# Cross entropy with label smoothing: one sum and one exponential per transfer, the first row completed on GpSimd, fewer instructions on VectorE and ScalarE

## The chip, the cores and the metric

One core of one Trainium2 chip. The time is device microseconds of one execution; medians of repeated runs are quoted. The profile is one execution on the chip, with times counted from the start of its span (first to last instruction of the kernel). The time is 1.7 to 1.9 us longer than the span (in every run but those of e2_old_end), since a closing sequence follows it. Engines: PE is TensorE (PEld its weight loads), DVE is VectorE, ACT is ScalarE, POOL is GpSimd, SP issues transfers.

## The reference, cut to what matters

```
batch, num_classes = 256, 32000          # logits fp32: 32.77 MB
log_probs = logits - max; log_probs -= log(sum(exp(log_probs)))
smooth_targets = smoothing/num_classes everywhere, + (1 - smoothing) at the label
return -sum(smooth_targets * log_probs)  # one number per row
```

The kernel needs, per row, the sum of the logits, the sum of their exponentials and the logit at the label. Each of 128 partitions holds two rows, handled one after the other. All 32.77 MB are read once.

## The kernel before

Each row is read in transfers of the widths below. Wide ones land in a ring of three buffers, narrow ones in buffers of their own. Every landed tile is cut into pieces of at most 4032 columns; each piece gets one sum on VectorE and one exponential with accumulation on ScalarE.

```
WIDTHS = (
    (8000, 8000, 8000, 8000),
    (8000, 6272, 4736, 3648, 2688, 2048, 1536, 1216, 1024, 832),
)
RING_MIN = 6000
PIECE = 4032
...
        if w >= RING_MIN:
            xt = ring.tile([P, max(WIDTHS[0])], FP32, name="xt", tag="xt")
        else:
            xt = tail.tile([P, w], FP32, name=name, tag=name)
...
    def sum_exps(xp, w: int, out: bass.AP) -> None:
        ja = turn.tile([P, PIECE], BF16, name="ja", tag="ja")   # three buffers
        nc.scalar.activation(out=ja[:, :w], in_=xp, func=AF.Exp, accum_out=out)
...
    # last row, at its last two tiles
        elif left == 1:
            nc.vector.tensor_tensor(
                out=done[1][:], in0=done[0][:], in1=pairs[0][:], op=ALU.add
            )
            nc.gpsimd.tensor_tensor(
                out=se_rest[:], in0=done[1][:, 1:2], in1=pairs[1][:, 1:2], op=ALU.add
            )
        elif left == 0:
            nc.vector.tensor_tensor(
                out=lin[:], in0=done[1][:, 0:1], in1=pairs[1][:, 0:1], op=ALU.add
            )
...
    finish(r, lin[:], elast[:], se_rest[:])   # logarithm, two transposes, combination
```

The softmax here doesn't subtract the row's maximum and nothing guards it: scores larger than these inputs give would overflow.

## Time and profile before

| | before |
|---|---|
| time, median | 85.11 us (85.00 to 85.12, 3 runs) |
| span of the profiled run | 83.23 us |
| instructions in the built program: VectorE, ScalarE, TensorE, GpSimd, SyncE | 78, 69, 50, 37, 37 |
| last tile landed, result landed, end of span | 78.92, 82.19, 83.23 us |

The instruction counts are from the built program, accumulator reads, waits and markers included. The landings are the semaphore records of the trace. Two lines of the page of the kernel before, busy time by engine and the busy tenths of the DMA engines in 40 slices of the span:

```profile
PE 8.0 (10%) x20; PEld 5.4 (6%) x20; DVE 38.7 (47%) x52; ACT 59.9 (72%) x45; POOL 4.6 (6%) x15
DMA  5999998996999699988999799999999999999500
```

No compute engine is busy for three quarters of the span, and the DMA engines are busy nearly everywhere but in the last two slices.

### The profile page before, as it was taken

Reading aid. Unit: us, or ns where it says so; the run is one execution under the profiler, and the core shown is the slowest. Engines: PE = TensorE matmul, PEld = TensorE weight load, DVE = VectorE, ACT = ScalarE, POOL = GpSimd, SP = SyncE. Lnnn points to the kernel's source line nnn. Section 1 sums busy time; section 2 is a strip of 40 time slices with the busy share of each in tenths; the row PEclk is TensorE's granted clock in tenths of the full one; section 3 lists DMA queues with packets and bytes.
Section 4 is the critical chain, followed back from the end, with each engine's and each line's share of the span. In section 5 each row is a group of like instructions: output and inputs, shape, how many; then the busy total and the mean of one; then the engine's idle time right before and its main releaser. Section 6 shows DMA issues by size and latency. Waiting matters only on the chain.

```text
span 83.2 us, 250 instructions
## 1 busy us (share of the span) xinstructions
PE 8.0 (10%) x20; PEld 5.4 (6%) x20; DVE 38.7 (47%) x52; ACT 59.9 (72%) x45; POOL 4.6 (6%) x15
## 2 busy tenths in 40 slices
PE   0000000000000000000001010000000000079960
PEld 0000000000000000000000000000000000067720
DVE  0000059600595009910497119923946754755760
ACT  5000059980699809993499909998999999999950
POOL 3202630010000000000000000000000000000010
PEclk9999999999999999999999999999999999999998
DMA  5999998996999699988999799999999999999500
GB/s 123 431 432 423 438 477 385 492 492 292 446 492 492 292 446 492 492 369 369 492 492 400 338 439 398 518 434 401 428 393 400 442 419 416 416 405 413 230 4 0
DMA packets 2259, 32.78 MB, mean 394 GB/s; under 512 B 337, under 2 KB 338, under 8 KB 850
## 3 DMA queue, kind: packets, MB, share of 16 engines
q1 hardware_dynamic: 2018, 30.72, 87.3%
q10 hardware_dynamic: 144, 2.05, 5.8%
q0 software_dynamic: 96, 0.00, 0.1%
q14 instruction: 1, 0.01, 0.0%
HBM read 32.77 MB, written 0.00 MB: 394 GB/s over the span
## 4 chain that ended last, share of the span: by engine, by line
DMA 59%; ACT 34%; DVE 2%; issue 1%; SPq 0%; PE 0%; ACTq 0%; DVEq 0%
DMA xt<-in_logits_dram 59%; ACT ja L189 34%; DVE jd L177 1%; SPq L171 0%; DVE lin_row L201 0%; PE lin_t L199 0%; DVE res L204 0%; DVE lin L288 0%; DVE done L281 0%; ACTq L189 0%; DVEq L204 0%
## 5 line engine op out<-in xcount | busy, mean ns | idle before, releaser
L189 ACT ACTIVATE ja<-xt 128x4000 bf16<-128x4000 f32 (+1 forms) x12 | 40.9, 3409 | 19.2 <-DMA xt<-in_logits_dram 19.2
L177 DVE SCALAR_TENSOR_TENSOR jd<-xt 128x2000 f32<-128x2000 f32 (+1 forms) x12 | 26.0, 2167 | 31.3 <-DMA xt<-in_logits_dram 31.1
L189 ACT ACTIVATE ja<-xl 128x2368 bf16<-128x2368 f32 (+7 forms) x9 | 16.6, 1839 | 0.0
L177 DVE SCALAR_TENSOR_TENSOR jd<-xl 128x1184 f32<-128x1184 f32 (+7 forms) x9 | 10.7, 1184 | 7.0 <-DMA xl<-in_logits_dram 6.8
L295 PE MATMUL warm<-xl,ident 128*128 128x256 f32 x16 | 6.7, 607 | 24.7 <-DMA xl<-in_logits_dram 24.7
L295 PEld LDWEIGHTS warm<-xl,ident 128*128 128x128 f32 x16 | 5.1, 324 | 26.2 <-DMA xl<-in_logits_dram 24.9
L199 PE MATMUL lin_t<-ident,both 128*1 128x128 f32 x1 | 0.4, 370 | 45.5 <-DVE both L226 45.5
L284 POOL TENSOR_TENSOR se_rest<-done,pair 128x1 f32<-128x1 f32 x1 | 0.4, 402 | 60.1 <-DVE done L281 60.1
L199 PEld LDWEIGHTS lin_t<-ident,both 128*1 128x1 f32 x1 | 0.1, 79 | 45.5 <-DVE both L226 45.5
L189 ACT ACTIVATION_READ_ACCUMULATOR ja<-xt 128x1 f32 x12 | 2.2, 187 | 0.0
L125 POOL DMA_INDIRECT gat<-in_logits_dram,flat_idx x2 | 2.0, 994 | 0.7 <-POOL ident masks.py:199 0.4
L92 ACT ACT_TABLE_LOAD x1 | 1.3, 1283 | 0.9 <-PEq L322 0.9
L189 ACT ACTIVATION_READ_ACCUMULATOR ja<-xl 128x1 f32 x9 | 1.6, 182 | 0.0
L177 DVE DVE_READ_ACCUMULATOR jd<-xt 128x1 f32 x12 | 1.0, 82 | 0.0
L201 DVE COPY lin_row<-lin_t 1x128 f32<-1x128 f32 x2 | 0.6, 278 | 0.8 <-PE lin_t L199 0.8
L204 DVE SCALAR_TENSOR_TENSOR res<-lin_row,lse_t 1x128 f32<-1x128 f32 x2 | 0.6, 276 | 0.8 <-PE lse_t L203 0.7
L229 DVE TENSOR_REDUCE both<-esum 128x1 f32<-128x8 f32 x1 | 0.2, 161 | 1.6 <-ACT ja L189 1.6
L148 POOL TENSOR_SCALAR xsum<-gat 128x1 f32<-128x1 f32 x2 | 0.4, 220 | 7.9 <-DMA gat<-in_logits_dram,flat_idx 7.9
L203 PE MATMUL lse_t<-ident,lse 128*1 128x128 f32 x2 | 0.6, 320 | 2.4 <-ACT lse L195 2.4
L105 POOL DMA_DIRECT2D lab<-in_labels_dram x1 | 0.8, 766 | 1.0 <-POOLq L322 1.0
L177 DVE DVE_READ_ACCUMULATOR jd<-xl 128x1 f32 x9 | 0.7, 83 | 0.0
L117 POOL TENSOR_TENSOR flat_idx<-rowoff,lab 128x2 int32<-128x2 int32 x1 | 0.2, 193 | 5.2 <-DMA lab<-in_labels_dram 5.2
(17 smaller groups left out, 2.9 us busy)
## 6 DMA issues: line engine op xcount, KB each, us to landing
xt<-in_logits_dram SPq DMA_DIRECT2D x4, 4000.0 KB, 21.6
xt<-in_logits_dram SPq DMA_DIRECT2D x1, 3136.0 KB, 19.2
xl<-in_logits_dram SPq DMA_DIRECT2D x1, 2368.0 KB
xt<-in_logits_dram SPq DMA_DIRECT2D x1, 2000.0 KB, 11.3
xt<-in_logits_dram ACTq DMA_DIRECT2D x1, 2000.0 KB, 13.0
xl<-in_logits_dram SPq DMA_DIRECT2D x1, 1824.0 KB, 28.3
xl<-in_logits_dram SPq DMA_DIRECT2D x1, 1344.0 KB, 31.1
xl<-in_logits_dram SPq DMA_DIRECT2D x1, 1024.0 KB, 33.1
```

The lines of the kernel that those rows point to most:

```text
L92: nc.scalar.add_instruction(mybir.InstLoadActFuncSet(name=nc.get_next_instruction_name(), act_func_set_id=tbl, ins=[], outs=[],))
L105: nc.gpsimd.dma_start(out=lab[:], in_=labels.bitcast(I32).rearrange("(p f) -> p f", p=P))
L125: nc.gpsimd.indirect_dma_start(out=gat[:, r : r + 1], out_offset=None, in_=logits[:], in_offset=bass.IndirectOffsetOnAxis(ap=flat_idx[:, r ...
L148: nc.gpsimd.tensor_scalar(out=xsum[:, 0:1], in0=gat[:, r : r + 1], scalar1=label_weight, scalar2=None, op0=ALU.mult,)
L177: return nc.vector.scalar_tensor_tensor(out=jd[:, :h], in0=xp[:, :h], scalar=1.0, in1=xp[:, h:w], op0=ALU.mult, op1=ALU.add, accum_out=out,)
L189: nc.scalar.activation(out=ja[:, :w], in_=xp, func=AF.Exp, accum_out=out)
L199: nc.tensor.transpose(out=lin_t[:], in_=lin, identity=ident[:])
L201: nc.vector.tensor_copy(out=lin_row[:], in_=lin_t[:])
L203: nc.tensor.transpose(out=lse_t[:], in_=lse[:], identity=ident[:])
L204: nc.vector.scalar_tensor_tensor(out=res[:, :, r : r + 1], in0=lin_row[:], scalar=-c_small, in1=lse_t[:], op0=ALU.mult, op1=ALU.add,)
L284: nc.gpsimd.tensor_tensor(out=se_rest[:], in0=done[1][:, 1:2], in1=pairs[1][:, 1:2], op=ALU.add)
L295: nc.tensor.matmul(warm[:], lhsT=ident[:], rhs=xt[:, i * WARM_COLS : (i + 1) * WARM_COLS], start=True, stop=True,)
```

## The change

The intent: fewer instructions. A whole transfer is one sum and one exponential, the first row's last steps move to GpSimd, and the two additions at the end of the second row become one. In the built program VectorE goes from 78 instructions to 61 and ScalarE from 69 to 54; TensorE has 56, GpSimd 42, SyncE 38. The diff, cut to its core:

```
-RING_MIN = 6000
-PIECE = 4032
-WARM_LEFT, WARM_COLS = 4, 256
+RING_MIN = 4736
+TURN_MAX = 3648
+WARM_LEFT, WARM_COLS = 5, 256
...
-            k = pieces[r][t]
-            for i in range(k):
-                xp = xt[:, i * (w // k) : (i + 1) * (w // k)]
-                sum_logits(xp, w // k, xsums[r][:, at + 1 : at + 2])
-                sum_exps(xp, w // k, esums[r][:, at : at + 1])
-                at += 1
...
+            sum_logits(xt, w, sums[:, 0, t : t + 1])
+            sum_exps(xt, w, sums[:, 1, t : t + 1])
+        while n > 1:
+            n //= 2
+            half = small.tile([P, 2, n], ...)
+            nc.gpsimd.tensor_tensor(
+                out=half[:], in0=sums[:, :, :n], in1=sums[:, :, n:], op=ALU.add
+            )
+            sums = half
...                     # logarithm on ScalarE; lin, scaled, loss on GpSimd
+        loss_t = row_of(loss[:], f"loss_t{r}")
+        nc.vector.tensor_copy(out=res[:, :, r : r + 1], in_=loss_t[:])
...                     # last row
-            nc.gpsimd.tensor_tensor(out=se_rest[:], ...)
-        elif left == 0:
-            nc.vector.tensor_tensor(out=lin[:], ...)
+        elif left < 2:
+            i = 1 - left
+            nc.vector.tensor_tensor(
+                out=done[i + 1][:], in0=done[i][:], in1=pairs[i][:], op=ALU.add
+            )
```

More of the change, by code (lines that the diff above doesn't have):

```diff
@@ L133 @@
     make_identity(nc, ident[:])
-    pieces = [[-(-w // PIECE) for w in ws] for ws in WIDTHS]
-    assert all(w % (2 * k) == 0 for ws, ks in zip(WIDTHS, pieces) for w, k in zip(ws, ks))
     label_weight = c_big / c_small
-    xsums, esums = [], []
+    xsum = small.tile([P, len(WIDTHS[-1]) + 1], FP32, name="xsum", tag="xsum")
+    esum = small.tile([P, len(WIDTHS[-1])], FP32, name="esum", tag="esum")
+    weighted = [
+        small.tile([P, 1], FP32, name=f"weighted{r}", tag=f"weighted{r}")[:]
+        for r in range(R - 1)
+    ] + [xsum[:, 0:1]]
     for r in range(R):
-        n = sum(pieces[r])
-        xsum = small.tile([P, n + 1], FP32, name=f"xsum{r}", tag=f"xsum{r}")
-        esum = small.tile([P, n], FP32, name=f"esum{r}", tag=f"esum{r}")
         nc.gpsimd.tensor_scalar(
-            out=xsum[:, 0:1],
+            out=weighted[r],
             in0=gat[:, r : r + 1],
@@ L154 @@
         )
-        xsums.append(xsum)
-        esums.append(esum)
     res = small.tile([1, P, R], FP32, name="res", tag="res")
@@ L172, in load, with sum_logits @@
         return xt
-    def sum_logits(xp, w: int, out: bass.AP):
+    def sum_logits(xt, w: int, out: bass.AP):
         h = w // 2
-        jd = junk.tile([P, PIECE // 2], FP32, name="jd", tag="jd")
+        jd = junk.tile([P, max(WIDTHS[0]) // 2], FP32, name="jd", tag="jd")
         return nc.vector.scalar_tensor_tensor(
             out=jd[:, :h],
-            in0=xp[:, :h],
+            in0=xt[:, :h],
             scalar=1.0,
-            in1=xp[:, h:w],
+            in1=xt[:, h:w],
             op0=ALU.mult,
@@ L185, in sum_logits, with sum_exps, row_of @@
         )
-    def sum_exps(xp, w: int, out: bass.AP) -> None:
-        ja = turn.tile([P, PIECE], BF16, name="ja", tag="ja")
-        nc.scalar.activation(out=ja[:, :w], in_=xp, func=AF.Exp, accum_out=out)
-    def finish(r: int, lin: bass.AP, se: bass.AP, se_rest) -> None:
-        lse = small.tile([P, 1], FP32, name=f"lse{r}", tag=f"lse{r}")
-        if se_rest is None:
-            nc.scalar.activation(out=lse[:], in_=se, func=AF.Ln)
-        else:
-            nc.scalar.activation(out=lse[:], in_=se, func=AF.Ln, bias=se_rest)
-        lin_t = psum.tile([1, P], FP32, name=f"lin_t{r}", tag=f"lin_t{r}")
-        nc.tensor.transpose(out=lin_t[:], in_=lin, identity=ident[:])
-        lin_row = small.tile([1, P], FP32, name=f"lin_row{r}", tag=f"lin_row{r}")
-        nc.vector.tensor_copy(out=lin_row[:], in_=lin_t[:])
-        lse_t = psum.tile([1, P], FP32, name=f"lse_t{r}", tag=f"lse_t{r}")
-        nc.tensor.transpose(out=lse_t[:], in_=lse[:], identity=ident[:])
-        nc.vector.scalar_tensor_tensor(
-            out=res[:, :, r : r + 1],
-            in0=lin_row[:],
-            scalar=-c_small,
-            in1=lse_t[:],
-            op0=ALU.mult,
-            op1=ALU.add,
-        )
+    def sum_exps(xt, w: int, out: bass.AP) -> None:
+        if w > TURN_MAX:
+            ja = junk.tile([P, max(WIDTHS[0])], BF16, name="ja", tag="ja")
+        else:
+            ja = turn.tile([P, TURN_MAX], BF16, name="jt", tag="jt")
+        nc.scalar.activation(out=ja[:, :w], in_=xt[:, :w], func=AF.Exp, accum_out=out)
+    def row_of(column: bass.AP, name: str):
+        row = psum.tile([1, P], FP32, name=name, tag=name)
+        nc.tensor.transpose(out=row[:], in_=column, identity=ident[:])
+        return row
     col = 0
     for r in range(R - 1):
-        at = 0
+        n = len(WIDTHS[r])
+        sums = small.tile([P, 2, n], FP32, name=f"sums{r}", tag=f"sums{r}")
         for t, w in enumerate(WIDTHS[r]):
@@ L218 @@
             col += w
-            k = pieces[r][t]
-            for i in range(k):
-                xp = xt[:, i * (w // k) : (i + 1) * (w // k)]
-                sum_logits(xp, w // k, xsums[r][:, at + 1 : at + 2])
-                sum_exps(xp, w // k, esums[r][:, at : at + 1])
-                at += 1
-        both = small.tile([P, 2], FP32, name=f"both{r}", tag=f"both{r}")
-        nc.vector.tensor_reduce(
-            out=both[:, 0:1], in_=xsums[r][:], axis=AX.X, op=ALU.add
-        )
-        nc.vector.tensor_reduce(
-            out=both[:, 1:2], in_=esums[r][:], axis=AX.X, op=ALU.add
-        )
-        finish(r, both[:, 0:1], both[:, 1:2], None)
+            sum_logits(xt, w, sums[:, 0, t : t + 1])
+            sum_exps(xt, w, sums[:, 1, t : t + 1])
+        while n > 1:
+            assert n % 2 == 0
+            n //= 2
+            half = small.tile([P, 2, n], FP32, name=f"half{r}_{n}", tag=f"half{r}_{n}")
+            nc.gpsimd.tensor_tensor(
+                out=half[:], in0=sums[:, :, :n], in1=sums[:, :, n:], op=ALU.add
+            )
+            sums = half
+        lse = small.tile([P, 1], FP32, name=f"lse{r}", tag=f"lse{r}")
+        nc.scalar.activation(out=lse[:], in_=sums[:, 1, :], func=AF.Ln)
+        lin = small.tile([P, 1], FP32, name=f"lin{r}", tag=f"lin{r}")
+        nc.gpsimd.tensor_tensor(out=lin[:], in0=sums[:, 0, :], in1=weighted[r], op=ALU.add)
+        scaled = small.tile([P, 1], FP32, name=f"scaled{r}", tag=f"scaled{r}")
+        nc.gpsimd.tensor_scalar(
+            out=scaled[:], in0=lin[:], scalar1=-c_small, scalar2=None, op0=ALU.mult
+        )
+        loss = small.tile([P, 1], FP32, name=f"loss{r}", tag=f"loss{r}")
+        nc.gpsimd.tensor_tensor(out=loss[:], in0=scaled[:], in1=lse[:], op=ALU.add)
+        loss_t = row_of(loss[:], f"loss_t{r}")
+        nc.vector.tensor_copy(out=res[:, :, r : r + 1], in_=loss_t[:])
     r = R - 1
     n = len(WIDTHS[r])
-    xsum, esum = xsums[r], esums[r]
     elast = psum.tile([P, 1], FP32, name="elast", tag="elast")
@@ L244 @@
     done = [
-        small.tile([P, 2], FP32, name=f"done{i}", tag=f"done{i}") for i in range(2)
+        small.tile([P, 2], FP32, name=f"done{i}", tag=f"done{i}") for i in range(3)
     ]
-    se_rest = small.tile([P, 1], FP32, name="se_rest", tag="se_rest")
-    lin = small.tile([P, 1], FP32, name="lin", tag="lin")
     warm = psum.tile([P, WARM_COLS], FP32, name="warm", tag="warm")
-    at = 0
     for t, w in enumerate(WIDTHS[r]):
@@ L254 @@
         col += w
-        k = pieces[r][t]
-        assert k == 1 or left > 2
-        for i in range(k):
-            xp = xt[:, i * (w // k) : (i + 1) * (w // k)]
-            part = sum_logits(
-                xp,
-                w // k,
-                xsum[:, at + 1 : at + 2] if left > 1 else pairs[1 - left][:, 0:1],
-            )
-            if left == 0:
-                to = elast[:]
-            elif left <= 2:
-                to = pairs[2 - left][:, 1:2]
-            else:
-                to = esum[:, at : at + 1]
-            sum_exps(xp, w // k, to)
-            at += 1
+        part = sum_logits(
+            xt, w, xsum[:, t + 1 : t + 2] if left > 1 else pairs[1 - left][:, 0:1]
+        )
+        if left == 0:
+            sum_exps(xt, w, elast[:])
+        elif left <= 2:
+            sum_exps(xt, w, pairs[2 - left][:, 1:2])
+        else:
+            sum_exps(xt, w, esum[:, t : t + 1])
         if left == 2:
@@ L274 @@
                 nc.vector.tensor_reduce(
-                    out=done[0][:, 0:1], in_=xsum[:, : at + 1], axis=AX.X, op=ALU.add
+                    out=done[0][:, 0:1], in_=xsum[:, : t + 2], axis=AX.X, op=ALU.add
                 )
                 nc.vector.tensor_reduce(
-                    out=done[0][:, 1:2], in_=esum[:, : at - 1], axis=AX.X, op=ALU.add
+                    out=done[0][:, 1:2], in_=esum[:, :t], axis=AX.X, op=ALU.add
                 )
-        elif left == 1:
+        elif left < 2:
+            i = 1 - left
             nc.vector.tensor_tensor(
-                out=done[1][:], in0=done[0][:], in1=pairs[0][:], op=ALU.add
-            )
-            nc.gpsimd.tensor_tensor(
-                out=se_rest[:], in0=done[1][:, 1:2], in1=pairs[1][:, 1:2], op=ALU.add
-            )
-        elif left == 0:
-            nc.vector.tensor_tensor(
-                out=lin[:], in0=done[1][:, 0:1], in1=pairs[1][:, 0:1], op=ALU.add
+                out=done[i + 1][:], in0=done[i][:], in1=pairs[i][:], op=ALU.add
             )
@@ L301 @@
                 )
-    finish(r, lin[:], elast[:], se_rest[:])
+    lse = small.tile([P, 1], FP32, name=f"lse{r}", tag=f"lse{r}")
+    nc.scalar.activation(out=lse[:], in_=elast[:], func=AF.Ln, bias=done[2][:, 1:2])
+    lin_t = row_of(done[2][:, 0:1], f"lin_t{r}")
+    lin_row = small.tile([1, P], FP32, name=f"lin_row{r}", tag=f"lin_row{r}")
+    nc.vector.tensor_copy(out=lin_row[:], in_=lin_t[:])
+    lse_t = row_of(lse[:], f"lse_t{r}")
+    nc.vector.scalar_tensor_tensor(
+        out=res[:, :, r : r + 1],
+        in0=lin_row[:],
+        scalar=-c_small,
+        in1=lse_t[:],
+        op0=ALU.mult,
+        op1=ALU.add,
+    )
     nc.sync.dma_start(
```

## The prediction

> **What bounds the kernel now.** I read the chain of waits first, then the table by stages, the timeline of the tail, and the transfers' issue-to-landing times. The chain of waits of the kernel before, in pieces (start, duration, what):
>
> ```profile
> 1.30 29.75 DMA xt<-in_logits_dram
> ...
> 38.30 19.17 DMA xt<-in_logits_dram
> ...
> 57.56 5.60 ACT ja L189 x3
> 63.20 4.33 ACT ja L189 x3
> 67.58 3.20 ACT ja L189
> ...
> 79.14 0.16 DVE done L281
> 79.31 0.52 DVE jd L177 x2
> ...
> 80.76 0.28 DVE res L204
> ```
>
> Read alone, this says that transfers bound the kernel until 57.5 us and the exponentials on ScalarE from there to 79.1. The busy times in stretches say something else about the second part (columns: stretch, length, busy us and count of PE, PEld, DVE, ACT, POOL, then clock, DMA share, GB/s):
>
> ```profile
> 11.00:50.00 39.00, 0.74 (x2) 0.16 (x2) 18.88 (x20) 28.80 (x17) 0.47 (x3) 1.00 1.00 430
> 57.50:79.00 21.50, 5.74 (x14) 4.57 (x15) 13.97 (x22) 21.44 (x20) 0.00 (x0) 1.00 0.96 399
> ```
>
> From 57.5 to 79 ScalarE is full (21.44 of 21.50 us), but the DMA share is still 0.96. Both are full, so the chain had to pick one. The timeline of the tail tells which:
>
> ```profile
> 67.45 0.18 ACT L189 ACTIVATION_READ_ACCUMULATOR ja<-xl 128x1 f32 x1
> 67.58 3.24 ACT L189 ACTIVATE ja<-xl 128x3648 bf16<-128x3648 f32 x1
> 67.59 2.06 DVE L177 SCALAR_TENSOR_TENSOR jd<-xl 128x1824 f32<-128x1824 f32 x1 [1.54 <-DMA xl<-in_logits_dram]
> ...
> 70.82 2.44 ACT L189 ACTIVATE ja<-xl 128x2688 bf16<-128x2688 f32 x1
> 70.83 1.56 DVE L177 SCALAR_TENSOR_TENSOR jd<-xl 128x1344 f32<-128x1344 f32 x1 [1.18 <-DMA xl<-in_logits_dram]
> ```
>
> VectorE had been idle for 1.54 and 1.18 us and waits for nothing but the landing, yet it starts within 0.01 us of ScalarE. Had tiles landed while ScalarE was still busy, VectorE would have started earlier. So each tile lands just as ScalarE comes free: the widths are tuned so that both run out together. The slack is visible: inside one tile the next exponential starts 0.09 us after the accumulator read of the last (65.29 to 65.38), at 67.45 it starts 0.13 after. The landings are also in the list of transfers (last number: issue to landing):
>
> ```profile
> xl<-in_logits_dram SPq DMA_DIRECT2D x1, 512.0 KB, 27.9
> xl<-in_logits_dram SPq DMA_DIRECT2D x1, 416.0 KB, 21.4
> ```
>
> The last one is issued at 57.49, so it lands at 57.49 + 21.4 = 78.9; ScalarE starts its exponential at 79.04. **DMA is the bound from 1.3 to 78.9 us**; after it come one 832-wide exponential (0.88), its accumulator read, the logarithm, transpose and store.
>
> **What the Trainium skill says.** "DMA: Bandwidth & Descriptors", Specifications, gives a fabric ceiling of 435 GB/s; this trace has 430 GB/s from 11 to 50 us at a share of 1.00, so there is nothing left to win in the stream. The same page, Queues, rings and completion order, says that each DMA engine consumes descriptors in ring order; the trace agrees: tiles land in the order issued. "ScalarE: Activation LUTs", What ACT_TABLE_LOAD costs, gives an ACTIVATE as 186 ns + 0.833 ns per column; for 4000 that is 3518 ns, and the trace has 3529. "Runtime: NRT & Kernel Launch", Instruction fetch mechanics, says the sequencer refills its instructions by its own DMA queue in 16 KiB blocks, mostly hidden. The trace has such packets, of 8192 bytes (not 16 KiB): in the DMA view from 79 us on,
>
> ```profile
> q14 instruction: 2, 0.02, 1.1%
> ```
>
> one starts at 79.83 inside the span, the other at 83.54, after the end of the span. Few instructions per engine, which the change aims at, can only pay through these.
>
> **The change part by part.**
> (1) One pair of operations per transfer. In tiles of 8000, 6272 and 4736 columns two exponentials and two sums become one each: seven fewer of each. One exponential saves 0.186 us fixed cost less the overlap, about 0.19 us a merge by the timeline (two 4000s: 21.58 to 28.73, 7.15; one 8000 by the formula: 6.85 + 0.1 = 6.95). VectorE saves about 0.15 a merge. For the five 8000s that lies beside the stream: ScalarE waits 19.2 us for landings already, and will wait 1.0 more. The first tile is the exception: its exponential now waits for both halves, starting near 13.1 instead of 11.33 and ending at 20.0 instead of 18.5; the transfer that needs its buffer is issued 1.5 us later, but the tile ahead lands at 21.6 and another full one is queued until 31.0, so the queue does not run dry. Cost 0.
> In the tail: the 6272 exponential starts at the landing, 57.56, takes 5.41 and frees ScalarE at 63.07 (was 63.17); the 4736 tile lands about 63.12 and starts at 63.20 as before. It ends 67.33, free at 67.42 (was 67.54); the next lands about 67.50. So both savings turn into waits for landings. From the 3648 tile on every operation is as before. Gain at the end: 0.
> (2) The 4736 tile moves into the ring (RING_MIN 4736), so its transfer and all behind it are issued when the fourth tile is released, about 47.6 instead of 38.7. Queued then: the rest of the fifth 8000 tile (landing 50.0) and the 6272 (landing 57.5), 10 us of work. Seven issues of 0.43 us fit. Cost 0.
> (3) First row completed on GpSimd. Removed from VectorE: two reductions and one combination; added to GpSimd: five operations of 128x1 to 128x4, 0.2 to 0.4 each by its own rows (TENSOR_SCALAR 220 ns, TENSOR_TENSOR 193 and 402), then one transpose (0.37) and a copy (0.28). From 47.5 that gives 49.5 to 50.4. VectorE's next sum may start 0.4 late at 50.4, in a stage where it works 4.4 of 7.5 us. Cost 0.
> (4) The end. The GpSimd addition se_rest goes; one VectorE addition makes both sums, and the logarithm waits for it. Before: se_rest ended 79.86, lin at 80.01, the last accumulator read at 79.98, logarithm at 80.07. The combined addition ends where lin did, so the logarithm starts between 80.07 and 80.12. VectorE's done at 79.14 shows 0.52 idle before it, although the 1216-wide exponential that it needs was complete at 78.01; no datum explains that, and it stands at about the 67th of 78 instructions in VectorE's built program. If it comes from instruction supply it goes (61 now): then lin is 0.2 earlier, and the final combination waits for the transposed logarithm alone, 80.69 instead of 80.76. Between +0.05 and -0.07.
> (5) Warm-up matmuls start with the tile before, 70.8 instead of 73.3, ten for eight: at about 0.78 each they end by 78.7 to 79.2; the last transposes should stay at 0.27 us. Cost 0.
> (6) Outside the span: 85.01 - 83.2 = 1.8 us in the profiled run. The fetch at 83.54 lies there, taking 0.57. If it disappears or comes earlier, at most 0.25 of that (an estimate; most overlaps the other engines' closing work).
> Sum: span 83.2 to about 83.15, outside 1.8 to about 1.75: near **84.95 us**.
>
> **The rivals.** *ScalarE is the bound of the tail*, as the chain says: then 2 merges x 0.19 = 0.4 us, 84.7. Against it: VectorE's simultaneous starts. *Late issue starves the queue* (2): each us of gap costs one us. Against it: two tiles queued at each release. If the issues were delayed behind the fifth tile's end, 85.5 to 86. *Instruction fetch matters more than I see*: fetches that collide with data stall an engine 0.5 us, as at 79.14; removing all would give 84.4 to 84.7. *A new wait at the end*: the combined addition waits for ScalarE's next-to-last sum; if it starts only with the last accumulator read (79.98), the end moves by +0.15, and cold transposes (0.37 for 0.27) would add 0.1 to 0.2: 85.3.
>
> **Range and chances.** Repeats of before lie within 0.12 us. The terms pull between -0.6 and +0.4, so 84.5 to 85.4 holds eight in ten. Two per cent is 1.7 us: none of the gains reaches it, since 77.6 us of stream stay; only a changed rate of the stream could. Faster 0.03, same 0.95, slower 0.02.
>
> **What would show it.** Right: landings at the same times (57.5, 63.1, 67.5, 78.9); ScalarE with new waits of about 0.1 before the 4736 and 3648 tiles; VectorE and ScalarE still starting together; DMA share about 1.00 from 11 to 50. Step 3 is wrong if the copy of the first row delays VectorE past 55; step 2 if the DMA share dips near 47 to 50; step 4 if the logarithm starts over 0.1 after the last accumulator read; step 6 if the time outside the span moves by over 0.25. The prediction is wrong if the stream itself ends at another time than 78.9.

## The result, and the profile after

| | before | after |
|---|---|---|
| first comparison, median (6 runs each) | 85.10 us (85.00 to 85.12) | 84.93 us (84.78 to 85.13) |
| ratio, 95% interval | | 0.9981 (0.9966 to 0.9997) |
| again (a1_after_again), median | 85.16 us (11 runs, 84.97 to 85.44) | 84.87 us (6 runs, 84.75 to 84.97) |
| ratio, 95% interval | | 0.9961 (0.9944 to 0.9978) |
| span of the profiled run | 83.23 us | 83.15 us |
| 8192-byte instruction packets from the start of the span on | at 79.83 and 83.54 us | none |

A ratio is the mean time of one kernel's fast runs over that of the kernel before in the same rounds, so it is not quite the ratio of the medians. The change is worth 0.2 to 0.4%: same at a threshold of 2%, and as predicted (84.95 us).

The page of the changed kernel, the same two lines as above:

```profile
PE 7.0 (8%) x23; PEld 5.0 (6%) x23; DVE 37.1 (45%) x35; ACT 58.8 (71%) x31; POOL 5.7 (7%) x19
DMA  5999999997999899989998998998999999999600
```

ScalarE and VectorE lost 14 and 17 of the instructions counted as busy, and 1.1 and 1.6 us of busy time, and the stream of loads looks as before. The chain of waits of the changed kernel, cut:

```profile
20.35 20.37 DMA xt<-in_logits_dram
...
48.17 19.52 DMA xl<-in_logits_dram
67.69 0.02 issue
67.72 7.63 ACT jt L188 x5
...
80.20 0.27 ACT lse L279
80.47 0.04 issue
80.52 0.28 PE lse_t L193
80.80 0.02 issue
80.83 0.28 DVE res L284
```

The DMA's part now reaches to 67.7 us instead of 57.5. The stream did not become slower. What changed is that ScalarE now really waits for the 4736 and 3648 tiles, so the chain follows the landings further. The table by stages (stretch, length, busy us and count of PE, PEld, DVE, ACT, POOL, clock, DMA share, GB/s) says the same:

```profile
11.00:50.00 39.00, 0.37 (x1) 0.08 (x1) 17.61 (x9) 28.05 (x9) 2.19 (x8) 1.00 1.00 432
57.50:79.00 21.50, 6.05 (x20) 4.80 (x20) 13.71 (x19) 21.05 (x15) 0.00 (x0) 1.00 0.97 404
```

The stream has 432 GB/s where it had 430. In the tail ScalarE has 0.39 us less work (21.44 to 21.05), and nothing ends earlier for it. The timeline of the tail shows where that work went:

```profile
63.10 0.19 ACT L188 ACTIVATION_READ_ACCUMULATOR ja<-xt 128x1 f32 x1
63.41 4.15 ACT L188 ACTIVATE ja<-xt 128x4736 bf16<-128x4736 f32 x1
63.42 2.62 DVE L173 SCALAR_TENSOR_TENSOR jd<-xt 128x2368 f32<-128x2368 f32 x1 [2.21 <-DMA xt<-in_logits_dram]
```

From the accumulator read (the instruction recorded after each exponential, which delivers its sum) to the next exponential there are 0.31 us now; before the same tile it was 0.12 (63.08 to 63.20 in the kernel before). The saved 0.2 us became a wait for the landing at 63.33, and VectorE again starts with ScalarE.

**Where the 0.2 to 0.3 us come from.** The profiled spans differ by only 0.08 us, but in the changed kernel's profiled run the whole stream came 0.19 us later (last tile at 79.11 for 78.92). That is variation between runs, not the change: the very first transfer, issued at 0.00 in both, had already landed 0.20 us later (11.50 for 11.30), and over all profiled runs with the full data the second tile landed between 21.55 and 22.15, and the later tiles kept that offset. So the comparison has to be made from the last landing on. The trace's records give:

| run | last tile to result landed | result landed to end of span | instruction packets |
|---|---|---|---|
| before | 3.26 us | 1.04 us | 79.83, 83.54 |
| e1_late_issue (before, one line changed) | 3.27 | 1.04 | 80.11, 83.82 |
| after | 3.15 | 0.90 | none |
| a1_after_again | 3.15 | 0.90 | none |
| e3_more_dve | 3.30 | 0.90 | 80.06 |
| e4_more_act | 3.15 | 1.04 | 83.57 |
| e2_old_end | 3.21 | 0.90 | none |
| e10_old_end_less_pool | 3.20 | 0.90 | none |
| e7_again | 3.08 | 0.90 | none |

From before to after: 0.11 us from the last landing to the result, 0.14 from there to the end of the span, together 0.25 us; the medians differ by 0.17 and 0.29. The experiments tell what each part is made of.

### The profile page after: what moved, and what is told of

It reads as the page before. It is cut to its first block, busy times and chain, and to the rows that moved or that the text cites. A ratio compares the mean times of both kernels' runs of the same rounds, so it can differ in the third digit from the quotient of the medians.

```text
span 83.2 us, 230 instructions
## 1 busy us (share of the span) xinstructions
PE 7.0 (8%) x23; PEld 5.0 (6%) x23; DVE 37.1 (45%) x35; ACT 58.8 (71%) x31; POOL 5.7 (7%) x19
## 3 DMA queue, kind: packets, MB, share of 16 engines
q10 hardware_dynamic: 144, 2.05, 5.8%
## 4 chain that ended last, share of the span: by engine, by line
DMA 64%; ACT 32%; issue 1%; SPq 0%; PE 0%; DVE 0%; ACTq 0%
DMA xt<-in_logits_dram 40%; DMA xl<-in_logits_dram 23%; ACT ja L188 17%; ACT jt L188 15%; SPq L167 0%; PE lse_t L193 0%; DVE res L284 0%; ACT lse L279 0%; ACTq L188 0%
## 5 line engine op out<-in xcount | busy, mean ns | idle before, releaser
L188 ACT ACTIVATE ja<-xt 128x8000 bf16<-128x8000 f32 (+2 forms) x7 | 43.9, 6276 | 20.1 <-DMA xt<-in_logits_dram 20.0
L173 DVE SCALAR_TENSOR_TENSOR jd<-xt 128x4000 f32<-128x4000 f32 (+2 forms) x7 | 27.7, 3954 | 33.6 <-DMA xt<-in_logits_dram 33.6
L188 ACT ACTIVATE jt<-xl 128x3648 bf16<-128x3648 f32 (+6 forms) x7 | 12.2, 1748 | 0.1
L173 DVE SCALAR_TENSOR_TENSOR jd<-xl 128x1824 f32<-128x1824 f32 (+6 forms) x7 | 7.9, 1125 | 5.2 <-DMA xl<-in_logits_dram 5.0
L270 PE MATMUL warm<-xl,ident 128*128 128x256 f32 x20 | 6.1, 471 | 21.4 <-DMA xl<-in_logits_dram 21.4
L188 ACT ACTIVATION_READ_ACCUMULATOR ja<-xt 128x1 f32 x7 | 1.3, 186 | 0.0
L188 ACT ACTIVATION_READ_ACCUMULATOR jt<-xl 128x1 f32 x7 | 1.3, 181 | 0.0
L146 POOL TENSOR_SCALAR weighted<-gat 128x1 f32<-128x1 f32 x1 | 0.8, 763 | 5.8 <-DMA gat<-in_logits_dram,flat_idx 5.8
```

Of the source, the lines that this page charges most:

```text
L146: nc.gpsimd.tensor_scalar(out=weighted[r], in0=gat[:, r : r + 1], scalar1=label_weight, scalar2=None, op0=ALU.mult,)
L173: return nc.vector.scalar_tensor_tensor(out=jd[:, :h], in0=xt[:, :h], scalar=1.0, in1=xt[:, h:w], op0=ALU.mult, op1=ALU.add, accum_out=out,)
L188: nc.scalar.activation(out=ja[:, :w], in_=xt[:, :w], func=AF.Exp, accum_out=out)
L270: nc.tensor.matmul(warm[:], lhsT=ident[:], rhs=xt[:, i * WARM_COLS : (i + 1) * WARM_COLS], start=True, stop=True,)
```

## The experiments

Three questions: does the stream really set the end (against the chain of waits, which named ScalarE); do the other parts of the change cost nothing, as predicted; and are the 0.25 us due to the missing instruction fetches (theory A) or to the shorter end of the dependency chain (theory B)?

### a1_after_again: the yardstick

The changed kernel unaltered, beside e2, e3 and e4 on one chip.

> The changed kernel again, beside the next three on one chip, as their yardstick. Both theories: ratio to the kernel before 0.998, near 84.9 us; no instruction packet after the start of the span.

Measured: 84.87 us, ratio 0.9961 (0.9944 to 0.9978), no instruction packet from the start of the span on. The small gain is there in a second set of runs.

### e6_half_exps: less work for ScalarE in the tail

```
-            sum_exps(xt, w, esum[:, t : t + 1])
+            sum_exps(xt, w // 2, esum[:, t : t + 1])
```

> The changed kernel, but the exponentials of the second row's first seven tiles (8000 to 1536 columns) read only half of their tile; wrong result on purpose. That takes 0.833 ns x 10464 columns = 8.7 us of ScalarE's work from 57.5 us on. If landings bound the tail (my theory): the time stays within 0.2 us of the changed kernel, 84.7 to 85.0, and ScalarE sits idle before each tile. If ScalarE bounds the tail, as the chain of waits of the kernel before says: 2 us or more faster.

Measured: 84.92 us (84.84 to 84.95), ratio 0.9977 (0.9953 to 1.0001). Its output is wrong, which doesn't matter for the time. The stage of the tail and one start in it:

```profile
57.50:79.00 21.50, 6.55 (x20) 5.11 (x20) 13.75 (x19) 12.65 (x15) 0.00 (x0) 1.00 0.97 405
...
63.31 2.18 ACT L188 ACTIVATE jt<-xt 128x2368 bf16<-128x2368 f32 x1 [2.75 <-DMA xt<-in_logits_dram]
```

ScalarE worked 12.65 us where it worked 21.05, sat idle 2.75 us before the tile of 4736 columns, and the time did not move. **Landings bound the tail**. The chain of waits of the kernel before, which put the tail on ScalarE, had picked one side of a tie.

### e5_less_data: less to load

```
-    (8000, 8000, 8000, 8000),
+    (7000, 7000, 7000, 7000),
...   (ring and scratch tiles keep their 8000 columns; row 2 still starts at column C)
```

> The changed kernel with 7000 columns for 8000 in each of the first row's four transfers; wrong result on purpose. 2.05 MB fewer; at the 432 GB/s of the stretch from 11 to 50 us that is 4.7 us. If the stream is the bound to the end: 80.2 us (79.9 to 80.5). If the tail has a bound of its own or a fixed rhythm of buffers: less of a gain, 82 or more.

Measured: 80.21 us (80.08 to 80.39), ratio 0.9426 (0.9400 to 0.9451). The sums leave out 4000 columns of each first row; the comparison's tolerance let that pass, but it is not the function asked for. The last tile landed at 74.39, and from there to the result it took 3.14 us as in the changed kernel. Taking 2.05 MB away saved 4.66 us against a1 (84.87 - 80.21; a1 ran on another chip, but the last landings, 79.09 and 74.39, differ by 4.70), 4.7 expected. The stream is the bound to its end, and the rest is a constant behind it.

### e1_late_issue: the change of the ring alone

```
-RING_MIN = 6000
+RING_MIN = 4736
```

in the kernel before.

> The kernel before with one line changed: the transfer of 4736 columns goes into the ring, so that it and all behind it are issued near 48 us instead of 39. My theory: no cost, 85.1 within 0.1, landings at the same times. Rival: the late issue makes the landings 0.2 us later, as they were in the changed kernel's profile (57.68 for 57.48, 79.11 for 78.92): 85.3.

Measured: 85.09 us, ratio 1.0001 (0.9981 to 1.0021). The queue's timeline in this run: two transfers into the ring from 38.61 on, the second of them held until a buffer came free, then six more.

```profile
38.61 9.81 SPq L171 DMA_DIRECT2D xt<-in_logits_dram  x2
48.48 2.80 SPq L171 DMA_DIRECT2D xl<-in_logits_dram  x6
```

The transfers behind the 6272 tile, all but the last two, are issued 9 to 10 us later than before, and it costs nothing, as the prediction's step 2 said. The rival saw the later landings of the changed kernel's profile as a result of this. This run's own profiled execution did have later landings too (last one 79.20), but at 85.32 us it was the slowest of its six; the median shows no loss.

### e8_row0_on_dve: the first row completed on VectorE

```
-            nc.gpsimd.tensor_tensor(out=half[:], ...)
+            nc.vector.tensor_tensor(out=half[:], ...)
...             (lin, scaled and loss in the same way)
```

> The changed kernel with the first row completed on VectorE (68 instructions there, 35 on GpSimd). Prediction's step 3: which engine completes the first row costs nothing by itself, 84.9; VectorE's next sum starts with the landing near 50.3. The instruction packet of VectorE comes back near or after the end of the span, since its 66th instruction now lies behind the last combination: up to 0.15 more, 85.0.

Measured: 84.88 us, ratio 0.9969 (0.9947 to 0.9991), the same as the changed kernel. The instruction packet came back at 83.74, behind the span, where it cost next to nothing (result landed to end of span 0.96 for 0.90). Which engine completes the first row is free. The changed kernel itself shows why, in its timeline between the two rows:

```profile
48.96 0.19 POOL L224 TENSOR_TENSOR loss<-scaled,lse 128x1 f32<-128x1 f32 x1
...
49.62 0.28 DVE L226 COPY res<-loss_t 1x128 f32<-1x128 f32 x1 [4.47 <-PE loss_t L193]
50.31 6.87 ACT L188 ACTIVATE ja<-xt 128x8000 bf16<-128x8000 f32 x1 [1.75 <-DMA xt<-in_logits_dram]
50.32 4.33 DVE L173 SCALAR_TENSOR_TENSOR jd<-xt 128x4000 f32<-128x4000 f32 x1 [0.42 <-DMA xt<-in_logits_dram]
```

The copy ends at 49.90, and VectorE still waits 0.42 us for the next tile.

### e3_more_dve and e4_more_act: the instructions put back, without their work

Tiny operations before the first tile lands, where both engines are idle: 17 memsets on VectorE (78 instructions again), or 15 exponentials of one column on ScalarE (69 again).

```
+    pad = small.tile([P, 17], FP32, name="pad", tag="pad")
+    for i in range(17):
+        nc.vector.memset(pad[:, i : i + 1], 0.0)
```

```
+    pad = small.tile([P, 15], FP32, name="pad", tag="pad")
+    for i in range(15):
+        nc.scalar.activation(out=pad[:, i : i + 1], in_=ident[:, i : i + 1], func=AF.Exp)
```

> The changed kernel with 17 tiny memsets on VectorE before the first tile lands, so that VectorE has as many instructions as in the kernel before (78). Theory A (the gain of 0.17 us is the missing instruction fetches): one packet of 8192 bytes on queue 14 comes back, in the span or just after it, and up to 0.1 to 0.2 us of the gain is lost: 85.0 to 85.1. Theory B (the gain is the shorter end of the chain, from the last landing to the store): 84.9, fetch or not. If the idle of 0.5 us before the addition of sums at 79.14 came from instruction supply, it comes back here.

> The changed kernel with 15 tiny exponentials on ScalarE before the first tile lands, so that ScalarE has as many instructions as in the kernel before (69). Theory A: the other of the two fetches comes back, and 0.1 to 0.2 us with it: 85.0 to 85.1. Theory B: 84.9. Tells which of the two packets of the kernel before belongs to which engine.

Measured on one chip: a1 84.87 us (84.75 to 84.97), e3 85.05 (84.96 to 85.19; ratio 0.9988, 0.9971 to 1.0005), e4 85.00 (84.87 to 85.14; ratio 0.9976, 0.9959 to 0.9994). The single ranges of the ratios overlap, but the traces show both losses at their place. In e3 the packet is back inside the span (first fence; packets of the instruction queue from 79 us on), and VectorE's sum of the last tile starts 0.25 us after that tile's landing at 78.99 (second fence) where the changed kernel needs 0.02:

```profile
q14 instruction: 1, 0.01, 0.4%
```

```profile
79.24 0.59 DVE L177 SCALAR_TENSOR_TENSOR jd<-xl 128x416 f32<-128x416 f32 x1 [0.29 <-DMA xl<-in_logits_dram]
```

In the kernel before the unexplained idle stood one instruction earlier in VectorE's order:

```profile
79.14 0.16 DVE L281 TENSOR_TENSOR done<-done,pair 128x2 f32<-128x2 f32 x1 [0.52 <-ACT ja L189]
```

In both traces this is the 64th instruction that is recorded for VectorE (the 67th of the built program, whose first few are not recorded). The idle stays at the count of instructions and not at the operation, and it is gone with 61 instructions. The label of the wait misleads both times: the exponential that L281 needs was complete at 78.02. A packet of 8192 bytes follows 0.7 to 0.8 us later (79.83 and 80.06). So the idle goes with the count of instructions; that the engine waits there for instruction supply is inferred from the packet, and no trace shows the wait itself. In e3 it delays the sums, with them the logarithm, and costs 0.15 us (3.30 for 3.15).

In e4 the packet is behind the span (83.57), as the second one of the kernel before. There ScalarE's last drain starts at 82.88 us, as in the kernel before (82.88), and at 82.63 in a1; every engine waits for it in the closing barrier, and the span ends 0.14 us later after the result has landed (1.04 for 0.90). So each packet belongs to one engine: the first to VectorE, the second to ScalarE. The count holds there too: the late drain is the 64th instruction recorded for ScalarE. The same is so in e1 (VectorE at 79.44, ScalarE at 83.17) and e8 (VectorE in the closing barrier, 83.06), and no run in which every engine stays below 64 recorded instructions has a packet.

### e2_old_end: the old additions at the end

```
-        elif left < 2:
-            i = 1 - left
-            nc.vector.tensor_tensor(
-                out=done[i + 1][:], in0=done[i][:], in1=pairs[i][:], op=ALU.add
-            )
+        elif left == 1:
+            nc.vector.tensor_tensor(out=done[1][:], in0=done[0][:], in1=pairs[0][:], op=ALU.add)
+            nc.gpsimd.tensor_tensor(out=done[2][:, 1:2], in0=done[1][:, 1:2], in1=pairs[1][:, 1:2], op=ALU.add)
+        elif left == 0:
+            nc.vector.tensor_tensor(out=lin1[:], in0=done[1][:, 0:1], in1=pairs[1][:, 0:1], op=ALU.add)
```

> The changed kernel with the end of the kernel before: the rest of the exponential sums added on GpSimd, the linear sum on VectorE. Theory A: 84.9, nothing at the end matters. Theory B (the logarithm started 0.09 us after the last accumulator read in the kernel before and 0.03 after in the changed one, because its last wait is now the instruction's own): the logarithm goes back to 0.08 to 0.09 after the read and 0.05 to 0.1 us are lost: 84.95 to 85.0.

Measured: 85.29 us (85.23 to 85.41), ratio 1.0013 (0.9997 to 1.0029), 0.42 us more than a1 beside it. Only 0.06 of that is where it was expected. Below are the last accumulator read and the logarithm, first in the kernel before, then in the changed one, then in e2:

```profile
79.83 0.15 ACT L189 ACTIVATION_READ_ACCUMULATOR ja<-xl 128x1 f32 x1
...
80.07 0.26 ACT L197 ACTIVATE lse<-elast,se_rest 128x1 f32<-128x1 f32 x1
```

```profile
80.02 0.15 ACT L188 ACTIVATION_READ_ACCUMULATOR jt<-xl 128x1 f32 x1
...
80.20 0.26 ACT L279 ACTIVATE lse<-elast,done 128x1 f32<-128x1 f32 x1
```

```profile
79.99 0.15 ACT L188 ACTIVATION_READ_ACCUMULATOR jt<-xl 128x1 f32 x1
...
80.23 0.26 ACT L286 ACTIVATE lse<-elast,done 128x1 f32<-128x1 f32 x1
```

From start to start it is 0.24, 0.18 and 0.24 us. In these programs an operation carries one wait itself, and a second wait is put into a separate instruction ahead of it (in the traces at 80.01 before, 80.03 after and 80.17 in e2). With the old end the last event to arrive (the accumulator read) is waited for by the separate instruction; with the new one it is the logarithm's own wait. That is worth 0.06 us. The rest, some 0.36 us, lies outside the span: the closing sequence, taken from the end of the span to the last record of the barrier's semaphore, took 2.35 us in e2's profiled run instead of 1.94 in a1's, with one step of the last barrier 0.52 us after the step ahead of it (84.90 to 85.42) where a1 has 0.10 (84.85 to 84.95), in a program in which GpSimd had 44 instructions. It is no accident of one run: in all six runs of e2 the time exceeds the span by 2.15 to 2.23 us, in those of a1 by 1.75 to 1.85.

### e9_more_pool and e10_old_end_less_pool: is that GpSimd's instruction count?

```
+    pad = small.tile([P, 2], FP32, name="pad", tag="pad")      # e9, on the changed kernel
+    for i in range(2):
+        nc.gpsimd.memset(pad[:, i : i + 1], 0.0)
```

```
-        nc.gpsimd.tensor_scalar(out=scaled[:], ...)            # e10, on e2
+        nc.vector.tensor_scalar(out=scaled[:], ...)
...
-        nc.gpsimd.tensor_tensor(out=loss[:], ...)
+        nc.vector.tensor_tensor(out=loss[:], ...)
```

> The changed kernel with two tiny memsets more on GpSimd near the start: 44 instructions there, as in the run with the old end, which closed 0.35 us later than the changed kernel although its span was the same (85.53 - 83.18 = 2.35 us for 1.94). Theory C: that came from GpSimd crossing a boundary of its instructions in the closing sequence: here too 0.3 to 0.5 us are lost outside the span, 85.2 to 85.4, with the span unchanged. Rival: it came from the addition on GpSimd late in the chain: 84.9.

> The run with the old end once more, but two operations of the first row on VectorE instead of GpSimd, so that GpSimd has 41 instructions. Theory C: the 0.35 us outside the span are gone, the 0.05 us of the later logarithm stay: 84.95. Rival (the late addition on GpSimd costs it): 85.3 again.

Measured: e9 84.93 us (ratio 0.9970, 0.9952 to 0.9987), closing sequence 1.91 us, so 44 instructions on GpSimd alone do not cost it. e10 84.92 us (ratio 0.9972, 0.9954 to 0.9989), closing 1.92 us, so the late addition on GpSimd alone does not either. Both single causes fall; the two together were not tried apart from e2, and what e2 lost outside the span stays **open**. What e10 does confirm is the loss inside the span: 3.20 us from the last landing to the result, as in e2 (3.21), against 3.15.

### e7_own_buffers and e7_again: no second wait in the tail

```
-    turn = ctx.enter_context(tc.tile_pool(name="turn", bufs=3))
+    turn = ctx.enter_context(tc.tile_pool(name="turn", bufs=1))
...
-            ja = turn.tile([P, TURN_MAX], BF16, name="jt", tag="jt")
+            ja = turn.tile([P, w], BF16, name=f"jt{w}", tag=f"jt{w}")
```

> The changed kernel with a buffer of its own for the exponentials of each of the last seven tiles, so that no exponential waits for an earlier one beside its landing. In the changed kernel's profile such exponentials (tiles of 3648 to 2048) start 0.02 us after the landing, those with two waits 0.08 after. Expected: the 1536, 1216 and 1024 tiles start 0.02 after landing as well, the last one 0.06 earlier, time 0.06 us less: 84.85. Rival: the start after landing does not depend on the second wait: no change.

> Own buffers for the last seven tiles' exponentials, again, on another chip: 84.75 to 84.85, ratio 0.995 to 0.997, so at least as fast as the changed kernel (0.9961 and 0.9981).

The observation that it rests on, from the traces' landing records and timelines:

| tile | landed, before | exponential starts after | landed, after | exponential starts after |
|---|---|---|---|---|
| 3648 | 67.50 | 0.08 us | 67.69 | 0.03 us |
| 2688 | 70.74 | 0.08 | 70.94 | 0.02 |
| 2048 | 73.22 | 0.08 | 73.42 | 0.02 |
| 1536 | 75.11 | 0.10 | 75.31 | 0.08 |
| 1216 | 76.62 | 0.08 | 76.82 | 0.08 |
| 1024 | 77.90 | 0.08 | 78.10 | 0.08 |

In the changed kernel the first three write into fresh buffers and wait for the landing alone; the others also wait for an earlier exponential's buffer, which puts the wait for the landing into a separate instruction. Measured: 84.70 us (ratio 0.9951, 0.9932 to 0.9970) and 84.81 (ratio 0.9956, 0.9938 to 0.9975). In e7_again the tiles of 1536, 1216 and 1024 columns start 0.04, 0.02 and 0.02 us after their landings. The last exponential starts at 79.14 with its tile landed at 79.09, and the result lands 3.08 us after the last tile, for 3.15: 0.07 us, as expected (3.10 in the profiled run of e7_own_buffers, the slowest of its seven). This is the fastest version: faster than the kernel before by 0.3 to 0.4 us; its lead on the changed kernel rests on the trace, since the intervals overlap (0.9956 against 0.9961 and 0.9981).

### What the 0.25 us are made of

Theory A (fetches) and theory B (a shorter end) both hold in part. From the last landing to the result: 3.26 us before, 3.21 with the old end and no fetch (e2), 3.15 after. So 0.06 is the place of the logarithm's last wait. The other 0.05 is a difference, not an experiment of its own; it is put down to VectorE's pause, which made the linear sum's copy late. From the result to the end of the span: 0.14 for ScalarE's late drain, which comes back with its packet in e4. That makes about 0.19 us for the two pauses that go with the packets and 0.06 for the waits. In e3 VectorE's pause costs more, 0.15, because it falls on the sum of the last tile, and the logarithm now waits for the addition behind it.

## Why the prediction was right

The time was predicted as 84.95 us and measured as 84.93 and 84.87. What was right is the bound and that most of the change costs and gains nothing. That the figure hits within 0.1 us is partly luck. The sum starts from one profiled run, 85.01 us, where the medians of that kernel are 85.07 to 85.16. It takes off about 0.1 (its own terms, 83.15 and 1.75, add up to 84.90), where 0.17 and 0.29 were measured. Its sign "wrong if the stream ends at another time than 78.9" is not met to the letter (79.11), by an offset that was there from the first landing on. By its own steps:

- **The bound.** DMA to the last landing, not ScalarE: shown by e6 (8.4 us of ScalarE's work removed in the tail, no change) and e5 (4.66 us for 2.05 MB). The clue that carried it, VectorE starting with ScalarE, holds in the traces: within 0.08 us at every tile but the last one or two.
- **Step 1, merged operations.** Predicted gain 0, with new waits of about 0.1 us before the 4736 and 3648 tiles. Right in kind, half the size: from accumulator read to next exponential it is now 0.31 and 0.25 us (67.47 to 67.72) where it was 0.12 and 0.13. The two merges in the tail saved 0.18 and 0.19 us (the 6272 columns took from 57.56 to 63.17 before and from 57.77 to 63.20 after), as the step's own figure for a merge says. Its tail sum came to half of that, since it compared ends with 0.1 added for the read of the accumulator (63.07, 67.42) with ends without it (63.17, 67.54). The first tile's exponential started at 13.37 and was over at 20.34 (13.1 and 20.0 predicted), without effect on the stream.
- **Step 2, later issue.** Cost 0: e1.
- **Step 3, first row on GpSimd.** Cost 0: e8 and the timeline. Its five operations took 0.19 to 0.21 us each, the low end of the estimate, so the copy ended at 49.90.
- **Step 4, the end.** Predicted between +0.05 and -0.07; measured -0.11. The step reckoned that the logarithm would start no earlier than before. In fact it starts 0.06 us sooner after the accumulator read (e2, e10), through the place of its last wait, which the prediction did not consider. The final combination follows its transpose by 0.04 us for 0.10: in the kernel before, the copy of the linear sum, late from the idle at 79.14, was complete only at 80.65, as was the transpose, and the combination waits for both. The suspicion about the idle at 79.14 holds as far as e3 can show it: it goes with VectorE's count of instructions, and a packet comes with it.
- **Step 5, warm-up matmuls.** Predicted to end at 78.7 to 79.2; they ended at 77.03 (at 77.0 to 78.2 over the runs with the full data and these ten). Ten took 6.05 us from 70.98 on, 0.61 each, where the step took 0.78 and the kernel before had 0.84 (eight in 6.68). The last transposes stayed at 0.27 us. No effect.
- **Step 6, the fetch at 83.54.** Its size was guessed at up to 0.25 us, 0.05 was put into the sum, and all of it outside the span. It was 0.14 us, inside the span: ScalarE's late drain holds the closing barrier (e4). Outside the span nothing changed (1.91 for before, 1.93 after).

Of the rivals, ScalarE as the bound fell with e6 and the starved queue with e1. The instruction fetch had a true core, but the rival put a kernel without fetches at 84.4 to 84.7 us; the changed kernel has none and takes 84.9. The new wait at the end did not come: the combined addition started at 79.83, before the last accumulator read.

## What to carry to other kernels

Where two engines start together at tile after tile, suspect that the landing starts them both; then, as here, work taken off either becomes a wait, whatever the chain of waits blames, and removing half of one engine's work is a cheap test of it. In a kernel bound by its stream, what is left to gain lies behind the last landing, so compare runs from there and not by their spans. There, look at which wait comes last: have it carried by the operation that needs it (a buffer of its own removes the second wait), and keep the short tail clear of the point in the instruction count at which an engine pauses (here the 64th recorded instruction of VectorE and of ScalarE).

## What the Trainium skill lacked or had wrong

- "Runtime: NRT & Kernel Launch", Instruction fetch mechanics: refills are given as 16 KiB blocks, mostly hidden. The packets here have 8192 bytes, and near the end of a short kernel one is not hidden: 0.15 us in the chain for VectorE (e3), 0.14 us in the closing barrier for ScalarE (e4). The engine's late instruction starts 0.65 to 0.82 us before the packet and is the 64th recorded for it in every run that has a packet (before, e1, e3, e4, e8).
- "Perfetto Trace Analysis", Per-engine timelines: it shows a wait of a VectorE or ScalarE instruction in a wait queue and that of a sequencer-only instruction at the sequencer, without what the difference costs. The runs show 0.02 to 0.04 us from landing to start where the operation carries the wait, and 0.08 to 0.10 where a separate instruction ahead of it does.
- No page has an account for the longer closing sequence of e2, 2.35 us for 1.94 with nearly the same span (83.18 and 83.14); the runs leave its cause open.
